# Weight splits spread over the sparse attention, and a rotary half that is exchanged by transfers

## The chip, the cores and the metric

The kernel runs on one core of a Trainium2 chip. A core has TensorE (PE, matrix products into PSUM), VectorE (DVE), ScalarE (ACT), GpSimd (POOL) and SyncE (SP, which here issues DMA transfers). The metric is the device time of one execution in microseconds; "before" stands at a median of 795.12 us over three runs (794.58 to 796.4).

## The reference, cut to what matters

The program is one decoder layer over 1024 tokens of width 1024: a modulated RMS norm, one input projection, two attention groups and an output projection. The second group is a multi-head latent attention with 8 heads; its queries come from a latent of rank 256, and 32 of each head's 96 query dimensions carry a rotary embedding:

```python
def rope(x, pos):
    half = x.shape[-1] // 2
    inv = ROPE_THETA ** (-jnp.arange(half, dtype=jnp.float32) / half)
    ang = pos.astype(jnp.float32)[..., None] * inv
    cos, sin = jnp.cos(ang)[:, :, None, :], jnp.sin(ang)[:, :, None, :]
    x1, x2 = xf[..., :half], xf[..., half:]
    return jnp.concatenate([x1 * cos - x2 * sin, x2 * cos + x1 * sin], axis=-1)

q = (rms_norm(c_q, q_norm_g) @ w_q_up).reshape(B, S, H, 64 + 32)
q_nope = q[..., :64]
q_rot = rope(q[..., 64:], positions)
```

Each output half of the rotary part needs both halves of x: one times the cosine, the other times the sine.

## The kernel before, in words

The kernel keeps float32 accuracy by splitting operands into a high and a low part (hi, and value − hi) and summing three products, hi·hi, hi·lo and lo·hi. A split is an ACT copy to the reduced type followed by a subtraction on DVE or POOL.

It runs in stages: modulation and input projection (to 352 us in the profile), the sparse attention (352 to about 532 us), the latent attention (to about 685 us) and the output projection.

The sparse attention is a loop over 74 pairs of blocks of 128 keys × 512 query columns (four heads). For pair i, `scores` (L994, L995, and L997 for a mask) fills a PSUM slot of tag `s` (three of them), `exps` takes two exponentials of it on ACT (E, float32, L1004; H, float16, L1005), `lows` subtracts them on DVE (L, L1010), and `weigh` multiplies with the values three pairs later (o, L937). A unit (128 tokens, one key group) has three branches, and after each branch `merge` scales the sum (cf, then mixn or tmp on DVE) and POOL adds it (L968). There are two PSUM banks for these sums, so the next branch waits for the merge before it.

Beside the pairs the loop prepares the latent attention with small jobs from three lists:
- `work`, from pair SIDE = 4 on, one each pair: two value/key weight splits (`kv_weights`), a bound on the values (`v_bound`, `v_scale`) and four query weight splits (`q_weights`). Each split job loads its weights into the one buffer of tag `raw`.
- `side`, from pair 36, every second pair: transposes of the latents and of the rotary tables.
- `late`, after pair 44 once `side` is empty: `k_rot`, `q_rot(0, 0)`, `q_rot(0, 1)`, `kq_first` twice, `q_rot_rows`, and the peaks of head 0 (`max_m`, L1256), which need the rotated rows.

`q_weights` stores the rotary columns of the weights twice: in their order, and with the two halves of 16 swapped. `q_rot(grp, hf)` (four heads, 512 tokens) multiplies the latents with both sets, twelve matmuls into the two halves of a PSUM slot (L1225). The first half times the cosine table (L1228), the second times the signed sine table (L1229), their sum on POOL (L1230), and its split into `qrs` (ACT L1231; L1232 on DVE for group 0 and on POOL for group 1) give the rotated rows, four heads × 32 rows × 512 tokens. The two products lie in a tile of the ring of three E tiles in the sparse attention, and in the one tile of tag `kqh` in the latent attention. `q_rot(1, 0)` and `q_rot(1, 1)` are placed at tasks 6 and 7 of the 48 tasks of the latent attention. `kq_first` uses the buffer `raw` and one of tag `rawl`; `kq_up` (L1155, L1156) uses `kqh` and `kql`, which transfers carry on to the heads' tiles.

Only TensorE's order is the order of the code. The instructions of the other engines, and the issues on SP's queue, are ordered by a planner that simulates the program with its own costs; a tile is reused when all that touched it is done. Each engine executes its own list in order, so an instruction that waits holds up those behind it.

Of the kernel before, what the change touches and what calls it, by code (L numbers as in the profile page):

```python
# [22 lines left out]
P = 128  # L23
# [4 lines left out]
H = 8  # L28
# [32 lines left out]
CMP_AT = (1, 12, 20, 28, 30, 44, 52, 60)  # L61
LAG = 3
SIDE = 4
SIDE_LAT = 36
LATE = 44
E_MIX = 8
# [28 lines left out]
def f32(ap):  # L95
    return ap.bitcast(F32)
# [11 lines left out]
def hybrid_block(ctx, tc, x, c, positions, ada_w, ada_b, norm_g, w_in, cmp_pos, cmp_k_w1, cmp_k_w2,  # L108
# [935 lines left out]
    cql = [rpool.tile([P, S], F32R, name=f"cql{k}") for k in range(2)]  # L1044
    wkh, wkl, wvh, wvl = [rpool.tile([P, H, 64], F32R, name=nm) for nm in ("wkh", "wkl", "wvh", "wvl")]
    wnh, wnl = [rpool.tile([P, 2, H, 64], F32R, name=nm) for nm in ("wnh", "wnl")]
    wrh, wrl = [rpool.tile([P, 2, 2, H, 32], F32R, name=nm) for nm in ("wrh", "wrl")]

    def split_w(hi, lo, src):
        nc.scalar.activation(hi, src, AF.Copy)  # L1050
        nc.vector.tensor_tensor(lo, src, f32(hi), op=ALU.subtract)
# [25 lines left out]
    def q_weights(k, i):  # L1077
        hs = slice(4 * i, 4 * i + 4)
        raw = raw_tile(f"wq{k}{i}")[:, :384].rearrange("p (h n) -> p h n", h=4)
        nc.sync.dma_start(raw, w_q_up[0, k * P:(k + 1) * P].rearrange("p (h n) -> p h n", h=H)[:, hs])  # L1080
        split_w(wnh[:, k, hs], wnl[:, k, hs], raw[:, :, :64])
        split_w(wrh[:, k, 0, hs], wrl[:, k, 0, hs], raw[:, :, 64:])
        for j in range(2):
            js = slice(j * 16, (j + 1) * 16)
            split_w(wrh[:, k, 1, hs, js], wrl[:, k, 1, hs, js], raw[:, :, 80 - j * 16:96 - j * 16])

    vb = npool.tile([P, 2], F32, name="vb")

# [127 lines left out]

    def q_rot(grp, hf):
        hs = slice(hf * 512, (hf + 1) * 512)
        pt = slot(f"qr{grp}_{hf}")
        for o in range(2):  # L1220
            n = 0
            for k in range(2):
                wh, wl = [w[:, k, o, grp * 4:grp * 4 + 4].rearrange("p h d -> p (h d)") for w in (wrh, wrl)]
                for a, b in ((wh, cqh[k]), (wh, cql[k]), (wl, cqh[k])):
                    nc.tensor.matmul(pt[:, o * 512:(o + 1) * 512], a, b[:, hs], start=(n == 0), stop=(n == 5))  # L1225
                    n += 1
        t1, t2 = pair_tile(f"qt{grp}{hf}")
        nc.vector.tensor_tensor(t1, pt[:, :512], tab_of[0][:, hs], op=ALU.mult)  # L1228
        nc.vector.tensor_tensor(t2, pt[:, 512:], tab_of[1][:, hs], op=ALU.mult)  # L1229
        nc.gpsimd.tensor_tensor(t1, t1, t2, op=ALU.add)  # L1230
        nc.scalar.activation(qrs[:, 0, hs], t1, AF.Copy)  # L1231
        (nc.gpsimd if grp else nc.vector).tensor_tensor(qrs[:, 1, hs], t1, f32(qrs[:, 0, hs]), op=ALU.subtract)  # L1232

    def v_up(t2):
        pt = slot(f"vu{t2}")
# [131 lines left out]
        nc.gpsimd.affine_select(causal_m[:, 896:], causal_m[:, 896:], pattern=[[-1, P]], compare_op=ALU.is_ge, fill=NEG,  # L1367
                                base=0, channel_multiplier=1)

    def pair_tile(name):  # L1370
        if "l" in mp:
            t = mp["l"].tile([P, 1024], F32, name=name, tag="kqh", bufs=1)
        else:
            t = npool.tile([P, 1024], F32, name=name, tag="E", bufs=EB)
        return t[:, :512], t[:, 512:]

    def junk_tile():
        if "l" in mp:
# [20 lines left out]
    with tc.manual_schedule(engines={mybir.EngineType.PE}):  # L1399
        for i in range(n_pairs + LAG + 2):  # L1400
# [11 lines left out]
            if i < n_pairs:  # L1412
                u = pairs[i][-1][0]
                before = len(todo)
                prep_next(u + 3)
                if u % G == 0 and u // G + 1 < NT and u // G + 1 not in cmr:
                    next_mask(u // G + 1)
                if i in KB_AT:
                    keys_b(kb_late, KB_CUT * P, S, KB_AT.index(i))
                if i >= SIDE and work:  # L1420
                    work.pop(0)()
                elif i >= SIDE_LAT and side:
                    if (i - SIDE_LAT) % 2 == 0:
                        side.pop(0)()
                elif i >= LATE and late and (len(late) > 6 or (i - LATE) % 2):
                    late.pop(0)()
# [164 lines left out]
```

## Time and profile before

| | before |
|---|---|
| median of three runs | 795.12 us |
| the profiled execution | 791.18 us |
| its span, first to last instruction | 789.4 us |
| PE / DVE / ACT / POOL busy | 731.7 / 576.9 / 389.7 / 228.1 us |
| mean granted TensorE clock | 0.976 |
| share of the chain that ended last: PE / DVE / DMA / ACT | 72 / 10 / 7 / 4% |

The profile is of one execution, and its rows add up to that one's own time. Busy time is the time with an instruction under way; matmuls are pipelined, so a row of a matmul is longer than the distance to the next. The chain of waits is followed back from the last instruction to what released each step; a row there is the time for which that instruction held up the end. In the timelines the brackets give the time for which the engine stood idle before the instruction and what ended it. The granted clock is a share of 2.4 GHz. An issue on SP's queue is the time in which SP works on one transfer; the data land later.

### The profile page before, as it was taken

To read this page: it belongs to the slowest core of one execution; us is meant where nothing else is said; L and a number is where in the kernel's file an instruction comes from. 1 tells how busy PE (TensorE), PEld (TensorE's weight loads), DVE (VectorE), ACT (ScalarE), POOL (GpSimd) and SP (SyncE) were. 2 spreads that over 40 slices of the span, in tenths; PEclk is the share of its full clock that TensorE was granted. 3 is DMA by queue.
4 is the path that set the end of the run, shared out by engine and by line. 5 is a ranking of instruction groups with operands and counts; after the bars stand their busy time and mean duration, and the time that the engine had idled before them with its cause. 6 is when DMAs were issued, how large, how long until landed. Compare 5 with 4: busy or idle time off the path is not lost.

```text
span 789.4 us, 17302 instructions
## 1 busy us (share of the span) xinstructions
PE 731.7 (93%) x6464; PEld 647.1 (82%) x6464; DVE 576.9 (73%) x1543; ACT 389.7 (49%) x691; POOL 228.1 (29%) x287
## 2 busy tenths in 40 slices
PE   3899999999999999997899999999698979999996
PEld 3889998998999999995677887777577868888885
DVE  3888835586688788879898989986487888654443
ACT  5545534233223232118899978985355666622112
POOL 3442522155222062404443221120110030054322
PEclk9799999999999999999999999999899999999998
DMA  8953313153431121113321123124315281345431
GB/s 302 300 162 107 94 51 86 61 141 91 137 93 55 31 58 42 35 56 93 80 51 40 33 56 81 36 62 100 77 28 122 58 224 56 145 137 174 152 115 54
DMA packets 62435, 76.48 MB, mean 97 GB/s; under 512 B 6342, under 2 KB 47113, under 8 KB 62351
## 3 DMA queue, kind: packets, MB, share of 16 engines
q1 hardware_dynamic: 57566, 70.91, 31.5%
q10 hardware_dynamic: 4784, 4.47, 1.7%
q8 instruction: 51, 0.84, 0.4%
q14 instruction: 34, 0.27, 0.1%
HBM read 48.33 MB, written 11.53 MB: 76 GB/s over the span
## 4 chain that ended last, share of the span: by engine, by line
PE 72%; DVE 10%; DMA 7%; issue 4%; ACT 4%; POOL 1%; SPq 1%; POOLq 0%; DVEq 0%; ACTq 0%
PE pj L589 23%; PE out L1523 11%; PE o L937 5%; PE pm L841 4%; PE s L994 3%; PE s L995 3%; PE mo L937 2%; PE ms L1297 2%; PE hid L642 2%; DVE L L1010 2%; PE kcT L321 2%; PE ms L1298 2%; PE ms L1299 2%; PE mm L1256 2%; PE qr L1225 1%
## 5 line engine op out<-in xcount | busy, mean ns | idle before, releaser
L589 PE MATMUL pj<-whi,hh 128*128 128x288 f32 (+2 forms) x544 | 161.4, 297 | 0.0
L589 PE MATMUL pj<-wlo,hh 128*128 128x288 f32 (+2 forms) x544 | 158.6, 292 | 0.0
L589 PE MATMUL pj<-whi,hl 128*128 128x288 f32 (+2 forms) x544 | 157.7, 290 | 0.0
L589 PEld LDWEIGHTS pj<-wlo,hh 128*128 128x128 f32 x544 | 102.5, 189 | 1.4
L589 PEld LDWEIGHTS pj<-whi,hh 128*128 128x128 f32 x544 | 102.6, 189 | 0.4
L589 PEld LDWEIGHTS pj<-whi,hl 128*128 128x128 f32 x544 | 102.2, 188 | 0.0
L1010 DVE TENSOR_TENSOR L<-E,H 128x1024 f16<-128x1024 f32 x74 | 92.0, 1243 | 12.8 <-ACT H L1005 10.9
L799 DVE CUSTOM_DVE_ANT_0 junk<-pm,maskw 128x256 bf16<-128x256 f32 (+3 forms) x160 | 77.9, 487 | 16.4 <-PE pm L841 4.4
L1004 ACT ACTIVATE E<-s 128x1024 f32<-128x1024 f32 x74 | 76.4, 1032 | 19.8 <-PE s L995 12.1
L937 PEld LDWEIGHTS <-H 128*128 128x128 f16 x1184 | 57.3, 97 | 30.1 <-issue 17.5
L968 POOL TENSOR_TENSOR mixn<-mixn,tmp 128x256 f32<-128x256 f32 x32 | 44.8, 1401 | 108.7 <-DVE tmp L967 101.8
L1005 ACT ACTIVATE H<-s 128x1024 f16<-128x1024 f32 x74 | 76.2, 1029 | 0.0
L841 PE MATMUL pm<-ka,qall 128*128 128x448 f32 (+5 forms) x208 | 67.2, 323 | 0.2 <-DVE mp L796 0.2
L937 PE MATMUL o<-v,H 128*128 128x65 f16 (+1 forms) x1056 | 60.1, 195 | 4.5 <-DVE mixn L964 4.5
L994 PE MATMUL s<-qa,ka 128*128 128x512 f32 x132 | 57.9, 439 | 3.0 <-ACT H L1005 2.6
L211 POOL TENSOR_TENSOR wlo<-wraw,whi 128x288 fp32r<-128x288 f32 (+2 forms) x64 | 51.4, 828 | 31.6 <-ACT whi L210 27.6
L937 PE MATMUL o<-v,L 128*128 128x65 f16 x528 | 56.8, 193 | 0.0
L937 PEld LDWEIGHTS <-L 128*128 128x128 f16 x592 | 55.7, 100 | 0.0
L1310 ACT ACTIVATE lat<-ms 128x1024 f32<-128x1024 f32 (+2 forms) x40 | 32.7, 817 | 34.2 <-PE ms L1302 16.3
L708 ACT ACTIVATE zt<-pj 128x288 f32<-128x288 f32 (+1 forms) x32 | 12.2, 385 | 74.5 <-PE pj L589 62.4
L1312 DVE TENSOR_TENSOR mL<-lat,mH 128x1024 f16<-128x1024 f32 (+2 forms) x40 | 39.7, 1004 | 5.8 <-ACT mH L1311 5.7
L995 PE MATMUL s<-qall,kb_early 128*128 128x512 f32 x108 | 43.3, 401 | 0.0
(380 smaller groups left out, 1863.5 us busy)
## 6 DMA issues: line engine op xcount, KB each, us to landing
ad<-in_ada_w_dram SPq DMA_DIRECT2D x32, 256.0 KB
wraw<-in_w_in_dram SPq DMA_DIRECT2D x20, 288.0 KB
x<-in_x_dram SPq DMA_DIRECT2D x8, 512.0 KB
gw<-in_ada_w_dram SPq DMA_DIRECT2D x32, 128.0 KB
qa<-qall SPq DMA_DIRECT2D x32, 128.0 KB
wor<-in_w_out_dram SPq DMA_DIRECT2D x16, 256.0 KB
xr<-in_x_dram SPq DMA_DIRECT2D x8, 512.0 KB
out_dram<-y SPq DMA_DIRECT2D x7, 512.0 KB
```

The source lines that it names most:

```text
L211: split.tensor_tensor(wlo[:, :width], raw[:, j, :width], f32(whi[:, :width]), op=ALU.subtract)
L589: nc.tensor.matmul(pt[:, :width], a[k][:, ts], b[:, :width], start=(n == 0), stop=(n == 23))
L799: nc.vector.tensor_tensor_reduce(out=junk[:, :w], in0=scores, in1=mask, scale=1.0, scalar=2.0 * NEG, op0=ALU.add, op1=ALU.max, accum_out=dst)
L841: nc.tensor.matmul(bank[:, :total_w], lhs, keys, start=True, stop=True)
L937: nc.tensor.matmul(po[:, c0:c0 + hi - lo], a[:n, qs], v[:, lo:hi], start=start and j == 0, stop=stop and j == 2, skip_group_check=True)
L968: nc.gpsimd.tensor_tensor(mv, mv, tmp, op=ALU.add)
L994: nc.tensor.matmul(dst, a, staged[u], start=True, stop=False)
L995: nc.tensor.matmul(dst, b, qc[u], start=False, stop=mk is None)
L1004: nc.scalar.activation(Et, pS, AF.Exp, scale=SC_NSA)
L1005: nc.scalar.activation(ph, pS, AF.Exp, scale=SC_NSA)
L1010: nc.vector.tensor_tensor(pl, Et, ph, op=ALU.subtract)
L1523: nc.tensor.matmul(po, a[:, kk], b[hf][k][:, cs.start - hf * 512:cs.stop - hf * 512], start=(n == 0), stop=(n == 23))
```

## The change

Two things are changed. The jobs of the list `work` are issued at every fourth pair (4, 8, ... 32) and no longer at every pair (4 to 11). And `q_rot` computes the rotary part of the queries once, with six matmuls and one set of weights; it multiplies it with the sine table into t2, exchanges neighbouring groups of 16 rows from t2 to t3 with eight transfers on SP's queue, multiplies the same PSUM values with the cosine table (into `qrs`' low half, as a place to keep them) and subtracts t3 on POOL. The sign of the sine table is thereby the other way round, hence the subtraction. In the sparse attention t2 lies in the buffer `raw` and t3 in one of tag `rawl`; in the latent attention both lie in `kqh`. The last subtraction is on DVE for both groups.

```diff
+SIDE_STEP = 4
...
-    wrh, wrl = [rpool.tile([P, 2, 2, H, 32], F32R, name=nm) for nm in ("wrh", "wrl")]
+    wrh, wrl = [rpool.tile([P, 2, H, 32], F32R, name=nm) for nm in ("wrh", "wrl")]
...
-        split_w(wrh[:, k, 0, hs], wrl[:, k, 0, hs], raw[:, :, 64:])
-        for j in range(2):
-            js = slice(j * 16, (j + 1) * 16)
-            split_w(wrh[:, k, 1, hs, js], wrl[:, k, 1, hs, js], raw[:, :, 80 - j * 16:96 - j * 16])
+        split_w(wrh[:, k, hs], wrl[:, k, hs], raw[:, :, 64:])
...
-        pt = slot(f"qr{grp}_{hf}")
-        for o in range(2):
-            n = 0
-            for k in range(2):
-                wh, wl = [w[:, k, o, grp * 4:grp * 4 + 4].rearrange("p h d -> p (h d)") for w in (wrh, wrl)]
-                for a, b in ((wh, cqh[k]), (wh, cql[k]), (wl, cqh[k])):
-                    nc.tensor.matmul(pt[:, o * 512:(o + 1) * 512], a, b[:, hs], start=(n == 0), stop=(n == 5))
-                    n += 1
-        t1, t2 = pair_tile(f"qt{grp}{hf}")
-        nc.vector.tensor_tensor(t1, pt[:, :512], tab_of[0][:, hs], op=ALU.mult)
-        nc.vector.tensor_tensor(t2, pt[:, 512:], tab_of[1][:, hs], op=ALU.mult)
-        nc.gpsimd.tensor_tensor(t1, t1, t2, op=ALU.add)
+        pt = slot(f"qr{grp}_{hf}")[:, :512]
+        n = 0
+        for k in range(2):
+            wh, wl = [w[:, k, grp * 4:grp * 4 + 4].rearrange("p h d -> p (h d)") for w in (wrh, wrl)]
+            for a, b in ((wh, cqh[k]), (wh, cql[k]), (wl, cqh[k])):
+                nc.tensor.matmul(pt, a, b[:, hs], start=(n == 0), stop=(n == 5))
+                n += 1
+        t2, t3 = turn_tiles(f"qt{grp}{hf}")
+        t1 = f32(qrs[:, 1, hs])
+        nc.vector.tensor_tensor(t2, pt, tab_of[1][:, hs], op=ALU.mult)
+        for r in range(0, P, 16):
+            nc.sync.dma_start(t3[r:r + 16], t2[r ^ 16:(r ^ 16) + 16])
+        nc.vector.tensor_tensor(t1, pt, tab_of[0][:, hs], op=ALU.mult)
+        nc.gpsimd.tensor_tensor(t1, t1, t3, op=ALU.subtract)
         nc.scalar.activation(qrs[:, 0, hs], t1, AF.Copy)
-        (nc.gpsimd if grp else nc.vector).tensor_tensor(qrs[:, 1, hs], t1, f32(qrs[:, 0, hs]), op=ALU.subtract)
+        nc.vector.tensor_tensor(qrs[:, 1, hs], t1, f32(qrs[:, 0, hs]), op=ALU.subtract)
...
-    def pair_tile(name):
+    def turn_tiles(name):
         if "l" in mp:
             t = mp["l"].tile([P, 1024], F32, name=name, tag="kqh", bufs=1)
-        else:
-            t = npool.tile([P, 1024], F32, name=name, tag="E", bufs=EB)
-        return t[:, :512], t[:, 512:]
+            return t[:, :512], t[:, 512:]
+        return raw_tile(name), npool.tile([P, 512], F32, name=name + "s", tag="rawl", bufs=1)
...
                 if i >= SIDE and work:
-                    work.pop(0)()
+                    if (i - SIDE) % SIDE_STEP == 0:
+                        work.pop(0)()
```

## Rows read from the trace of the kernel before

**Rows 1.** Stretches: busy us of each engine (instructions), granted clock share, DMA share, GB/s.
```profile
core 0: us, PE busy (x) PEld busy (x) DVE busy (x) ACT busy (x) POOL busy (x), PEclk, DMA share, GB/s
...
399.00:437.00 38.00, 37.99 (x574) 30.15 (x573) 33.80 (x64) 36.64 (x39) 15.10 (x15) 1.00 0.18 46
463.00:480.00 17.00, 16.82 (x147) 13.45 (x144) 13.87 (x18) 10.78 (x13) 4.88 (x4) 1.00 0.13 36
...
560.00:575.00 15.00, 15.00 (x112) 12.76 (x112) 10.88 (x15) 5.28 (x8) 3.43 (x3) 0.89 0.29 69
```

**Rows 2.** Chain of waits, 398 to 456 us: shares of it by line.
```profile
by line: PE o L937 37.0%; PE s L994 25.0%; PE s L995 22.3%; PE s L997 8.1%; PE latT L1095 4.6%; PE tab L1104 1.9%; PE nmT L855 1.3%; issue 0.0%
```

**Rows 3.** ACT in time: start, duration, line, tile; in brackets idle time and releaser.
```profile
362.61 1.08 ACT L1004 ACTIVATE E<-s 128x1024 f32<-128x1024 f32 x1
...
387.65 0.42 ACT L1050 ACTIVATE wnh<-wq 128x256 fp32r<-128x256 f32 x1
...
388.47 1.00 ACT L1004 ACTIVATE E<-s 128x1024 f32<-128x1024 f32 x1
...
390.28 1.02 ACT L1004 ACTIVATE E<-s 128x1024 f32<-128x1024 f32 x1
...
393.23 1.01 ACT L1004 ACTIVATE E<-s 128x1024 f32<-128x1024 f32 x1
...
399.36 1.02 ACT L1004 ACTIVATE E<-s 128x1024 f32<-128x1024 f32 x1 [0.44 <-PE s L995]
...
436.55 1.02 ACT L1004 ACTIVATE E<-s 128x1024 f32<-128x1024 f32 x1
```

**Rows 4.** Chain of waits, 362 to 399 us: start, duration, engine, tile, line.
```profile
378.70 0.88 DVE wnl L1051
379.58 0.47 DVE wrl L1051 x3
...
381.47 0.43 DVE mixn L964
...
389.86 2.53 DMA wq<-in_w_q_up_dram
...
392.75 0.57 ACT wrh L1050 x3
```

**Rows 5.** Chain of waits, whole span: the matmuls of the four rotary calls.
```profile
463.67 2.75 PE qr L1225 x12
468.35 2.83 PE qr L1225 x12
...
563.63 2.83 PE qr L1225 x12
...
569.74 2.87 PE qr L1225 x12
```

**Rows 6.** Instructions on tile qt: count, then shortest, median and longest duration in ns.
```profile
L1230 POOL TENSOR_TENSOR qt<-qt x4: 1279/1284/1287, 467.9 to 574.1; 128x512 f32<-128x512 f32 x4
L1231 ACT ACTIVATE qrs<-qt x4: 634/634/635, 469.5 to 576.4; 128x512 fp32r<-128x512 f32 x4
```

**Rows 7.** Line 1215: issue of one transfer on SP's queue, ns.
```profile
L1215 SPq DMA_DIRECT2D qh<-qrs x6: 553/577/657, 506.1 to 619.1; - x6
```

**Rows 8.** Chain of waits: from the end of an issue to its landing.
```profile
583.52 1.77 DMA qh<-mrow
```

**Rows 9.** SP's queue in time, near the first rotary call.
```profile
464.84 2.91 SPq L859 DMA_DIRECT2D qall<-mr  x4
```

**Rows 10.** TensorE in time: the first peak matmuls.
```profile
486.31 0.71 PE L1256 MATMUL mm<-qall,qall 96*128 96x512 f32 x2
```

**Rows 11.** DVE in time: first product of the second call of group 1.
```profile
572.70 0.69 DVE L1228 TENSOR_TENSOR qt<-qr,lat 128x512 f32<-128x512 f32 x1 [0.41 <-issue]
```

**Rows 12.** Waits, 350 to 690 us: total us, times, longest.
```profile
DVE kql L1156 <- DMA kl<-kql: 12.8, 3, 10.2
...
ACT kqh L1155 <- DMA kh<-kqh: 9.7, 1, 9.7
```

## The prediction

> **What bounds the kernel now.** I read the views from the coarse to the fine: the busy shares of stretches, then the chain of waits of each stretch that the change touches, then single engines in time there. Three stretches matter, and each has another limit. From 362 to 399 us (pairs 4 to 17 of the sparse attention) a pair takes long: E of pair 4 starts at 362.61, of pair 17 at 399.36 and of pair 36 at 436.55 [rows 3], so 13 pairs take 36.75 us, while the next 19 take 37.19 (1.96 each). At the later pace the 13 would take 25.4, so 11.3 us are lost here. The chain there runs largely over DVE and shows where the weight splits sit on it: wnl and wrl for 0.88 + 0.47 us, directly ahead of a merge (mixn at 381.47), and later the load wq, 2.53 us, followed by the ACT copies [rows 4]. From 398 to 456 us the chain is TensorE alone [rows 2], while ACT is nearly full too, 36.64 of 38 us, and DVE is at 33.80 [rows 1]. From 463 to 480 and from 560 to 575 us the rotary calls stand on the chain with their twelve matmuls each, 2.75, 2.83, 2.83 and 2.87 us [rows 5]; TensorE is busy 16.82 of 17 and 15.00 of 15 us there, DVE 13.87 and 10.88 [rows 1].
>
> **The weight splits.** Eight small jobs were issued at pairs 4 to 11; they go to pairs 4, 8, ... 32, so the last is issued ahead of pair 36, where the turns begin: those and the rotary calls keep their pairs. The four query-weight jobs move out of the slow stretch, to pairs 20 to 32. Each loses two small ACT copies and two small DVE subtractions, because the exchanged columns are no longer stored.
> Gain in the slow stretch, by what the chain and ACT show: the merge at 381.47 comes 0.88 + 0.47 = 1.35 us earlier [rows 4]; the ACT copies between 387.65 and 388.47 go, 0.82; and E of pair 14, at 393.23, could follow the two exponentials that begin at 390.28, which like the two from 388.47 take 1.81, so at 392.09, 1.14 earlier [rows 3]. Sum 3.3 us. What is late next is DVE's own series of merges. At least the first term, 1.35, should come; at most the whole pieces of the chain, 1.35 + 2.53 + 0.57 = 4.45 [rows 4]. I take 3.3, since its terms are read where E really starts. The other value-weight jobs stay within the stretch, only later: 0.
> Cost in the middle stretch: of the 0.82 us that a job's four copies take on ACT, two copies remain, with 256 and 128 of 512 columns: 0.41 by their count, 0.62 by columns; I take 0.53. A pair takes 1.96 and two exponentials 1.81, so four pairs leave 0.6 us free: it just fits. DVE has 38 − 33.80 = 4.2 us [rows 1] for four such pairs of subtractions; even at 1.35 each (5.4) little would stick out. The load has four pairs' time and doesn't wait for its buffer. Bounds 0 to 4 × 0.53 = 2.1 if nothing is hidden; I take 0.3. Net of the splits: −3.0.
>
> **The rotary calls.** Each loses six of twelve matmuls, half of its row: (2.75 + 2.83)/2 = 2.79 us in the sparse attention and (2.83 + 2.87)/2 = 2.85 in the latent attention [rows 5]. DVE keeps two products a call, and the two POOL subtractions of group 1 become DVE's. New is the exchange between the products and the addition: eight transfers of 16 rows. The trace has no such transfer; the nearest row, 32 rows of twice the length, occupies SP 0.577 us [rows 7], the lower bound being no issue beyond one, the upper the 0.73 of the issues in [rows 9] (2.91/4). Eight are 4.6 us (0.6 to 5.8), since one queue issues one after the other, and the last lands 1.77 us after its issue [rows 8]. An exchange therefore puts some 6.4 us between product and subtraction.
> Queued behind it: on SP the query loads of later units, on POOL the merge additions, on ACT the split behind which exponentials stand, and on DVE the next call's first product, because both calls now write one buffer (raw, later kqh) instead of a ring of three. Behind that product stand L and the merges, for which TensorE waits.
> *First pair of calls.* The matmuls of the first end by about 465. SP is taken until 464.84 + 2.91 = 467.75 [rows 9], so the issues end at 472.4 and the last lands at 474.1. Then the second product may be written: 474.1 + 0.69, issues to 479.4, landing 481.2, POOL 1.28, ACT 0.63 [rows 6], 483.1; the row transfer 0.58 + 1.77 gives 485.5. The first peak matmul, which needs these rows, runs now at 486.31 [rows 10]. So the longer path is just hidden, with 0.8 us to spare. But the latent key and query splits that follow use the same buffer, free only at 481.2, and hold their PSUM slots meanwhile, so the 2.79 us that TensorE no longer needs become waits for slots. I take 0, between −2.8 and +6.1 (next part).
> *Second pair.* Matmuls from 563.63 to 565.0, product to 565.7, issues to 570.3, landing 572.1, POOL to 573.4. Only then can the next call's first product start, now at 572.70 [rows 11]: 0.7 later instead of earlier. Scores and peaks of the tasks between still come up to 1.4 earlier. I take −0.5, between −2.85 and +5.1.
> The sum: −3.3 + 0.3 + 0 − 0.5 = −3.5. On the profiled execution, 791.18 us (span 789.4 and 1.8 around it), that is 787.7. The median of the timed runs is 795.12, 3.9 above the profiled one; carried over, 791.6.
>
> One page of the Trainium skill, "DMA: Bandwidth & Descriptors" (section "Issuing engines are not separate DMA queues"), says that the sequencer's time to start a DMA is usually small beside the DMA itself. By this trace it is not: 8 × 0.577 against 1.77. By the page an exchange would take little over one landing, and that is the first rival's case.
>
> **The rivals.** *The matmuls pay in full.* If issues are short (the lower bound) an exchange takes 0.6 + 1.77 = 2.4 us, less than one pair and a call, so no slot is held and both halves count: −3.0 − 2.79 − 2.85 = −8.6, 786.5. For it: TensorE is full in both stretches [rows 1]. Against: every SP issue shown is near 0.6 [rows 7].
> *The transfers block an engine (slower).* Only TensorE's order is written by hand; elsewhere a planner orders instructions by its own estimate of when they can run. If it reckons an exchange shorter than it is, the product or split that needs it stands ahead of L or an exponential and blocks them. For it: DVE stood 10.2 and ACT 9.7 us behind transfers out of this very buffer [rows 12]. Against: between SP's issues there is room, and the planner can place these instructions late. Price: 4.6 us a call; in the first pair 9.2 less the 17 − 13.87 = 3.1 us that DVE has free [rows 1], 6.1. Then −3.0 + 6.1 − 0.5 = +2.6, 797.7; with the second pair as well, 9.2 less 15 − 10.88 = 4.1, so 5.1, it is +8.2, 803.3. It turns the sign once the blocking passes some 3.5 us beyond what is free.
> *Nothing to be measured.* The splits come back: only 1.35 is won early and 1.6 of the 2.1 is paid in the middle, the calls come out even: +0.2, 795.3. For it: ACT has 0.6 us free for 0.53. Against: DVE's load in the slow stretch really falls.
>
> **How the numbers follow.** Forecast 0.40, paid in full 0.19, blocked 0.24, nothing 0.17. The likeliest gives 791.6, of itself 789.3 to 793.5. The range reaches to 785.5 (the full payment and 1 us of drift) and to 799.5 (past the first blocked case); outside lie the doubly blocked one and a part of the full payment's spread, under 0.2. About 0.2%, 1.6 us, is what a measurement can tell from no change. Faster by more: 0.58 (forecast without 0.02, paid in full, a little of the last case's spread); within: 0.18; slower: 0.24.
>
> **What would show it.** Right: pair 17 starts its E some 3 us earlier after pair 4, the chain from 398 to 456 us is still TensorE, SP shows eight issues of some 0.58 us a call, each call has six matmuls, and the first peak matmul stands within 1 us of its old distance from the first rotary call. Wrong would be: ACT or DVE rows with idle time ended by the transfers t3; waits of TensorE on the key and query splits longer by more than 3 us; splits of wq on the chain between 400 and 437 us; or issues far shorter than 0.5 us.

## The result and the profile after

The changed kernel takes 804.40 us (median of 16 runs, 796.03 to 808.69) against 796.69 us for the kernel before in the same session; the ratio is 1.0067, 95% interval [1.0043, 1.0091]. It is slower, by some 5.3 us, where 3.5 us less were forecast. The ratios here leave out disturbed runs, the medians hold all. The profiled execution of after took 802.65 us: its span is 800.9 at a mean granted clock of 0.959, where the one of before had 789.4 at 0.976.

I compare stage by stage, by the moments at which ACT begins the exponential E of a pair. The rows are ACT in time in the kernel after (start, duration, line, tile; in brackets the idle time before and what ended it): pairs 4, 17, one weight split, then pairs 36, 47, a key split with the high part H behind it, and pair 54.

```profile
360.21 1.08 ACT L1005 ACTIVATE E<-s 128x1024 f32<-128x1024 f32 x1
...
393.35 1.03 ACT L1005 ACTIVATE E<-s 128x1024 f32<-128x1024 f32 x1 [0.83 <-PE s L996]
...
406.33 0.42 ACT L1051 ACTIVATE wnh<-wq 128x256 fp32r<-128x256 f32 x1 [0.90 <-DMA wq<-in_w_q_up_dram]
...
432.39 1.03 ACT L1005 ACTIVATE E<-s 128x1024 f32<-128x1024 f32 x1
...
458.56 1.02 ACT L1005 ACTIVATE E<-s 128x1024 f32<-128x1024 f32 x1
...
478.17 0.59 ACT L1201 ACTIVATE kqh<-kq 64x512 fp32r<-64x512 f32 x1 [1.58 <-DMA qt01s<-qt]
...
479.71 1.02 ACT L1006 ACTIVATE H<-s 128x1024 f16<-128x1024 f32 x1
...
486.65 1.03 ACT L1005 ACTIVATE E<-s 128x1024 f32<-128x1024 f32 x1 [1.34 <-PE s L998]
```

From pair 4 to 17 it is 33.14 us (36.75 in [rows 3]): 3.61 won. From 17 to 36 it is 39.04 (37.19 in [rows 3]): 1.85 lost, of which 0.90 stands in the row at 406.33, where the split waits for its load. From 47 to 54, the stretch with the first two rotary calls, it is 28.09, where the kernel before takes 26.12: 1.97 lost. Pairs 47 and 54 in ACT's trace of before:

```profile
462.72 1.03 ACT L1004 ACTIVATE E<-s 128x1024 f32<-128x1024 f32 x1
...
488.84 1.03 ACT L1004 ACTIVATE E<-s 128x1024 f32<-128x1024 f32 x1 [1.03 <-PE s L997]
```

SP's queue, the chain of waits and TensorE, all of after, show how; first the queue (start, time, line, tiles, count; the last row spans both calls of the latent attention, with SP's wait between them):

```profile
460.68 2.91 SPq L860 DMA_DIRECT2D qall<-mr  x4
463.69 4.99 SPq L1228 DMA_DIRECT2D qt00s<-qt  x8
...
471.55 5.20 SPq L1228 DMA_DIRECT2D qt01s<-qt  x8
...
565.14 13.97 SPq L1228 DMA_DIRECT2D qt<-qt  x16
```

Then the chain from 462 to 486 us (start, duration, what):

```profile
467.46 0.59 SPq L1228
...
468.09 1.98 DMA qt00s<-qt
...
470.23 1.30 POOL qrs L1230
...
476.16 1.94 DMA qt01s<-qt
...
478.22 1.28 POOL qrs L1230
...
479.52 0.69 DVE kql L1202
...
484.13 1.22 PE mm L1256 x2
```

Where the chain of before was TensorE and its rotary matmuls [rows 5], it is now issue after issue, a landing, POOL, and the same once more: the second call's issues begin only at 471.55, when POOL has read the first call's halves. The second call's product, which writes the buffer that the first exchange reads, stands on DVE behind that exchange's landing (470.07), though its matmuls end by 464.3. Its PSUM slot, one of three, is held until then:

```profile
470.19 0.69 DVE L1226 TENSOR_TENSOR qt<-qr,lat 128x512 f32<-128x512 f32 x1
```

Behind the second exchange stand the key splits: ACT's kqh waits 1.58 us for the landing, and H, which TensorE's next scores need, stands behind kqh on ACT. TensorE in time shows it:

```profile
459.26 0.48 PE L1222 MATMUL qr<-cqh,wrh 128*128 128x512 f32 x1
...
470.67 0.73 PE L1178 MATMUL kq<-cqh,wnh 128*128 128x512 f32 x2 [1.27 <-ACT H L1006]
476.64 0.50 PE L995 MATMUL s<-qa,ka 128*128 128x512 f32 x1 [1.28 <-ACT H L1006]
480.78 0.50 PE L995 MATMUL s<-qa,ka 128*128 128x512 f32 x1 [2.19 <-ACT H L1006]
484.13 1.22 PE L1256 MATMUL mm<-qall,qall 96*128 96x512 f32 x2 [0.16 <-DVE rtab L1202]
```

These are three waits for H, 4.74 us. The middle one is not of the exchange: before has it at the same place, with 1.34 us. The other two make 3.46, more than the 2.79 us of matmuls that the two calls no longer have. TensorE in before, the first rotary matmul and that wait:

```profile
463.43 0.48 PE L1225 MATMUL qr<-cqh,wrh 128*128 128x512 f32 x1
...
482.07 0.50 PE L994 MATMUL s<-qa,ka 128*128 128x512 f32 x1 [1.34 <-ACT H L1005]
```

The first peak matmul of after stands at 484.13, 24.87 us behind the first rotary matmul; before it was 22.88 (from 463.43 to 486.31 in [rows 10]).

In the latent attention the chain of after shows the second pair of calls:

```profile
573.04 0.61 DVE qt L1226
...
578.53 1.94 DMA qt<-qt
...
580.59 2.37 POOL qrs L1230
...
582.98 0.64 ACT qrs L1231
...
583.64 0.69 DVE qrs L1232
584.33 0.07 DVE hl L1270
...
584.55 0.37 PE mn L1272
```

The second call's product starts at 572.96 on DVE, 11.24 us behind the first rotary matmul (561.72). Before it was 9.23 (from 563.47, by its trace, to 572.70 in [rows 11]). Its subtraction at 583.64, which POOL did before, now stands on DVE ahead of hl, for which the peaks' transposition mn waits on TensorE. Two TensorE rows of after name the idle time, and the stretch 565 to 590 us is then set beside the same stretch of before (columns as in [rows 1]):

```profile
574.30 1.32 PE L1256 MATMUL mm<-kh,qh 96*128 96x512 f32 x3 [2.28 <-DVE qrs L1229]
...
584.55 0.37 PE L1272 MATMUL mn<-ident,hl 128*16 128x128 f32 x1 [2.36 <-DVE mcf L1320]
```

After:

```profile
565.00:590.00 25.00, 20.36 (x147) 17.06 (x146) 18.80 (x39) 9.62 (x13) 3.62 (x2) 0.75 0.19 43
```

Before:

```profile
565.00:590.00 25.00, 23.27 (x226) 19.35 (x225) 21.04 (x44) 12.03 (x17) 5.65 (x4) 1.00 0.10 23
```

TensorE is busy for 20.36 us with 147 matmuls, where before it did 226 in 23.27; the granted clock is 0.75, so a good part runs at 1.2 GHz in place of 2.4. The sixth, ninth and twelfth exponential of the latent attention begin on ACT in after at:

```profile
560.61 0.92 ACT L1310 ACTIVATE mixm<-ms 128x896 f32<-128x896 f32 x1 [2.00 <-PE ms L1302]
...
578.22 1.02 ACT L1310 ACTIVATE lat<-ms 128x1024 f32<-128x1024 f32 x1 [1.94 <-PE ms L1299]
...
592.42 0.92 ACT L1310 ACTIVATE lat<-ms 128x896 f32<-128x896 f32 x1 [4.15 <-PE ms L1302]
```

and in before at:

```profile
562.59 0.92 ACT L1310 ACTIVATE mixm<-ms 128x896 f32<-128x896 f32 x1 [2.00 <-PE ms L1302]
...
578.25 1.02 ACT L1310 ACTIVATE lat<-ms 128x1024 f32<-128x1024 f32 x1 [1.23 <-PE ms L1299]
...
587.11 0.92 ACT L1310 ACTIVATE lat<-ms 128x896 f32<-128x896 f32 x1 [2.31 <-DVE peak L1260]
```

From the sixth to the ninth 17.61 us pass (15.66 before), from the ninth to the twelfth 14.20 (8.86). The two profiled spans differ by 11.5 us; 6.19 of these lie behind the twelfth (208.48 us to the end in after, 202.29 in before), where both kernels have the same code, at a granted clock of 0.96 and 0.98.

### The profile page after: what moved, and what is told of

Its sections match the earlier page's. It is cut to its first block, busy times and chain, and to the rows that moved or that the text cites. A ratio compares the mean times of both kernels' runs of the same rounds, so it can differ in the third digit from the quotient of the medians.

```text
span 800.9 us, 17297 instructions
## 1 busy us (share of the span) xinstructions
PE 737.8 (92%) x6440; PEld 653.1 (82%) x6440; DVE 581.1 (73%) x1537; ACT 388.7 (49%) x683; POOL 224.7 (28%) x285
## 4 chain that ended last, share of the span: by engine, by line
PE 72%; DVE 10%; DMA 6%; issue 4%; ACT 4%; SPq 3%; POOL 1%; POOLq 0%; DVEq 0%; ACTq 0%
PE pj L590 24%; PE out L1523 11%; PE o L938 4%; PE pm L842 4%; PE mo L938 3%; PE s L995 3%; PE kcT L322 2%; PE s L996 2%; DVE L L1011 2%; PE mm L1256 2%; PE ms L1297 2%; PE hid L643 2%; PE ms L1298 2%; PE ms L1299 2%; SPq L1228 2%
## 5 line engine op out<-in xcount | busy, mean ns | idle before, releaser
L969 POOL TENSOR_TENSOR mixn<-mixn,tmp 128x256 f32<-128x256 f32 x32 | 42.1, 1316 | 111.5 <-DVE tmp L968 104.9
L1260 DVE CUSTOM_DVE_ANT_0 junkm<-mm,lat 128x1024 bf16<-128x1024 f32 (+7 forms) x48 | 36.2, 753 | 16.5 <-PE mm L1256 16.2
```

Source lines behind the costliest of these rows:

```text
L969: nc.gpsimd.tensor_tensor(mv, mv, tmp, op=ALU.add)
```

## The experiments

All kernels ran against the kernel before on the same chip. The table gives, from each profile, the stages just named (E of pairs 4 to 17, 17 to 36, 47 to 54; latent exponentials 6 to 12), then the mean granted clock of the runs compared, what a kernel takes more or less than before *at like clock*, and the ratio. Like clock comes from a straight line through the 311 runs of the 18 kernels that the comparisons use, with one slope and a level for each kernel: 0.01 of mean clock goes with 5.2 us, 1.7 us scatter about the line, so with 12 runs a level is known to about 1 us, and that of e3, from five runs, to about 1.6. It orders what was seen; it doesn't prove that the clock is the cause. The line pools the runs of before from five chips, whose mean clocks go from 0.964 to 0.969; those beside after's own ratio are not among them. (The expectations of the ninth and later runs quote it from fewer runs.) A dash: no stage is read from that profile.

| kernel | 4-17 | 17-36 | 47-54 | lat. 6-12 | clock | at like clock | ratio [95%] |
|---|---|---|---|---|---|---|---|
| before | 36.75 | 37.19 | 26.12 | 24.52 | 0.966 | 0 | 1 |
| after | 33.14 | 39.04 | 28.09 | 31.81 | 0.960 | +3.2 | 1.0067 [1.0043, 1.0091] |
| e1 splits only | 34.26 | 39.61 | 26.12 | 24.98 | 0.964 | -0.5 | 0.9978 [0.9952, 1.0005] |
| e2 exchange only | 36.09 | 37.51 | 28.52 | 27.66 | 0.963 | +2.9 | 1.0021 [0.9982, 1.0060] |
| e3 no transfers | 33.79 | 38.75 | 23.75 | 23.70 | 0.968 | -5.6 | 0.9883 [0.9834, 0.9932] |
| e4 exchange, latent only | - | - | - | - | 0.966 | -0.7 | 0.9969 [0.9929, 1.0009] |
| e5 exchange, sparse only | 33.42 | 40.20 | 27.89 | 25.76 | 0.965 | +2.3 | 1.0024 [0.9988, 1.0059] |
| e6 two queues | 33.71 | 38.72 | 26.97 | 28.97 | 0.958 | +1.5 | 1.0036 [1.0006, 1.0067] |
| e7 own tile, latent | 33.85 | 38.98 | 29.01 | 26.73 | 0.959 | +2.5 | 1.0056 [1.0019, 1.0093] |
| e8 shuffle | 33.43 | 39.57 | 24.91 | 26.10 | 0.962 | -1.4 | 1.0002 [0.9965, 1.0039] |
| e9 twelve matmuls | 33.45 | 38.80 | 30.12 | 30.24 | 0.961 | +4.7 | 1.0073 [1.0043, 1.0103] |
| e10 shuffle from PSUM | - | - | - | - | 0.965 | -2.7 | 0.9968 [0.9937, 0.9999] |
| e11 loads ahead | 35.35 | 38.04 | 26.12 | 25.72 | 0.970 | +1.8 | 0.9981 [0.9952, 1.0009] |
| e12 unread | 33.13 | 38.94 | 28.40 | 26.16 | 0.962 | -0.7 | 1.0004 [0.9970, 1.0037] |
| e13 own buffers | 34.12 | 39.15 | 27.26 | 26.75 | 0.961 | -0.9 | 1.0047 [1.0012, 1.0083] |
| e14 own buffers, unread | 33.77 | 38.83 | 25.51 | 23.82 | 0.962 | -1.7 | 1.0037 [1.0003, 1.0071] |
| e15 shuffle, loads ahead | 34.04 | 37.80 | 24.84 | 23.62 | 0.964 | -3.7 | 0.9985 [0.9951, 1.0019] |
| e16 issues only | 35.74 | 37.19 | 26.12 | 25.30 | 0.962 | 0.0 | 1.0052 [1.0015, 1.0089] |

**e1, the splits alone.** The kernel before with this:

```diff
+SIDE_STEP = 4
...
-                    work.pop(0)()
+                    if (i - SIDE) % SIDE_STEP == 0:
+                        work.pop(0)()
```

> The kernel before with the work list at every fourth pair, the rotary calls as before. Waiting theory (the exchanges of group 1 cost the time): faster than before by about 1.8 us, the gain that the changed kernel shows at pair 36 of the sparse attention against its first pair, or a little less, since the swapped copies are still split in the middle stretch; ratio 0.997 to 0.999. Splits theory (spreading the splits costs the time): slower, ratio 1.003 or more.

What four pairs win (2.49) the middle gives back (2.42), with all four copies kept. The ratio, 0.9978, is in the range of the waiting theory: the splits are not what makes the change slower.

**e2, the exchange alone.** The kernel after with `SIDE_STEP = 1`.

> The changed kernel with the work list at every pair again. Waiting theory: slower than before, by the loss of the changed kernel and about the 1.8 us that the spread of the splits gave, less about 1 us for the copies no longer made: ratio 1.006 to 1.010. Splits theory: equal to before or faster, ratio 0.996 to 1.001.

The stretch from 47 to 54 is that of after (28.52), the latent one, 27.66, lies between before and after. The ratio, 1.0021, is below what was expected and its interval holds no change too: inconclusive by time, though at like clock it is 2.9 us over before.

**e3, no transfers.** The second table's product is subtracted unexchanged, so the rotary part is left out of what is computed:

```diff
-        for r in range(0, P, 16):
-            nc.sync.dma_start(t3[r:r + 16], t2[r ^ 16:(r ^ 16) + 16])
...
-        nc.gpsimd.tensor_tensor(t1, t1, t3, op=ALU.subtract)
+        nc.gpsimd.tensor_tensor(t1, t1, t2, op=ALU.subtract)
```

> The changed kernel without the eight transfers of each call: t2 itself is subtracted, so the rotated rows are not the right ones and the exchange is left out. Waiting theory: the loss goes, and the halved matmuls pay at least in part, 2 to 8 us faster than before: ratio 0.990 to 0.998. Theory that fewer matmuls let TensorE's clock fall: the clock in the latent attention stays as low as in the changed kernel (0.72 to 0.76 between 560 and 600 us), ratio 1.003 or more.

This is the decisive run: 1.2% under before, even below the waiting theory's range, and 1.8% under after. Pairs 47 and 54 in its trace:

```profile
460.12 1.02 ACT L1005 ACTIVATE E<-s 128x1024 f32<-128x1024 f32 x1
...
483.87 1.02 ACT L1005 ACTIVATE E<-s 128x1024 f32<-128x1024 f32 x1 [1.16 <-PE s L998]
```

23.75 us: the six matmuls a call pay 2.37 us there, near the 2.79 counted for them, and the exchange takes 28.09 - 23.75 = 4.34 away (4.14 to 5.26 by the profiles of e2, e5 and e7, whose calls there are those of after). The other theory wanted a granted clock of 0.72 to 0.76 between 560 and 600 us; with six matmuls a call and no transfers it is 1.00 (0.74 in after, 0.96 in before).

**e4 and e5, the exchange in one pair of calls.** The other pair keeps the code of before, with its exchanged weight columns:

```diff
+        if grp not in EXCH:
+            return q_rot_two(grp, hf)
```

> The changed kernel with the exchange in group 1 alone (latent attention); group 0 (sparse attention) with twelve matmuls and both sets of weights as before. Waiting theory: as slow as the changed kernel or 1 to 2 us better, ratio 1.004 to 1.008, with the low clock between 560 and 600 us. If the exchange in the sparse attention were the cause: equal to before or faster, 0.996 to 1.001.

> The exchange in the calls of the sparse attention only; the two calls in the latent attention keep twelve matmuls, two products and POOL as before (the splits of their weights keep the exchanged columns). Theory 1 (the waiting behind the exchanges of the sparse attention is the larger part of the loss, 4.4 us in the stretch from pair 47 to pair 54, and the kernel with the exchange in the latent attention alone came out at 0.997): ratio to the kernel before 1.003 to 1.008, pair 47 to 54 about 28 us, the latent attention's ninth E again 49 us after the last sparse one. Rival (the latent attention is where it is lost, for 2.1 us there and the low clock behind it): ratio 0.995 to 1.000. If neither half alone is slower than before, the loss needs both: ratio also under 1.001, with the stretch from 47 to 54 at 28 us all the same.

e4 missed: with the exchange in the latent attention alone the time is that of the splits alone (-0.7 and -0.5 at like clock). e5 confirms the place: 27.89 us from 47 to 54, and 2.8 us more than e1 at like clock, though its ratio is below the 1.003 of theory 1. But neither is clearly slower than before, and their mean clocks are near that of before; only both together are slower, with a lower clock.

**e6, two queues.** `(nc.scalar if r % 32 else nc.sync).dma_start(...)` in place of `nc.sync.dma_start(...)`.

> Of the eight transfers of each exchange every second one is issued by ACT's queue in place of SP's. Theory 1 (the serial issue on one queue, 8 x 0.59 us, is the larger part of the 6.7 us between product and subtraction): the issues take 2.4 us in place of 4.7, the path 4.3, the stretch from pair 47 to 54 falls from 28.1 to about 25 us, ratio 0.998 to 1.002. Rival (ACT is nearly full there, so four issues of some 0.6 us in each call cost ACT the 2.4 us that SP saves, and an issue that waits for the product blocks the exponentials behind it): ratio 1.005 to 1.012 and ACT's idle time behind the issues grows.

SP's issues took 2.52 us for four in the first call, but only about 1.1 us of the stretch come back; the time lies between both expectations, above that of before.

**e7, own tile in the latent attention.** The second call takes the tag kql, the first keeps kqh.

> The second rotary call of the latent attention writes its products into another buffer than the first (that of the low key and query parts), so that its product need not wait until the first call's subtraction is done. Theory 1 (the two calls in series, on one buffer, make the 2.1 us by which the ninth latent E is late, and the low clock behind it): second call's product about 4 us earlier, SP's issues then directly behind those of the first, ninth E at 49.5 to 50 us, ratio 1.001 to 1.004. Rival (SP's queue keeps the order anyway and the later splits wait for the other buffer in the same way): ninth E at 51, ratio 1.005 to 1.009.

Rows of the sixth and ninth latent exponential:

```profile
570.15 0.92 ACT L1310 ACTIVATE mixm<-ms 128x896 f32<-128x896 f32 x1 [2.01 <-PE ms L1302]
...
583.74 1.02 ACT L1310 ACTIVATE lat<-ms 128x1024 f32<-128x1024 f32 x1 [1.24 <-PE ms L1299]
```

13.59 us in place of 17.61: the shared buffer is what delays the ninth, as theory 1 said. The time hardly moved all the same (1.0056, in the rival's range); from the ninth to the twelfth 13.14 us pass, at a granted clock of 0.79 in that trace from 584 to 600 us.

**e8 and e10, a shuffle in place of the transfers.** The first permutes the product, the second the matmuls' result, and POOL then multiplies:

```diff
-        for r in range(0, P, 16):
-            nc.sync.dma_start(t3[r:r + 16], t2[r ^ 16:(r ^ 16) + 16])
+        nc.vector.stream_shuffle(t3, t2, [r ^ 16 for r in range(32)])
...
+        nc.vector.stream_shuffle(t3, pt, [r ^ 16 for r in range(32)])
+        nc.gpsimd.tensor_tensor(t2, t3, tab_of[1][:, hs], op=ALU.mult)
+        nc.gpsimd.tensor_tensor(t1, t1, t2, op=ALU.add)
```

> The halves are exchanged by one VectorE shuffle a call (each block of 32 partitions permuted) in place of the eight transfers; all else as in the changed kernel. Theory 1 (the loss is the 6.7 us path of issues and landing, nothing in the six matmuls): by the products' 0.69 us a shuffle costs about 0.7 us of DVE, four of them 2.8 at most on the path, so ratio 0.988 to 0.994, near the kernel without an exchange (0.988), pair 47 to 54 at 24 to 25 us, and TensorE's clock without the drop after 560 us. Rival 1 (fewer matmuls and the splits' new places lose the time, the transfers only show it): ratio above 1.000. Rival 2 (the shuffle is much slower than a product, 2 us or more): DVE the bound there, ratio 0.996 to 1.002.

> The exchange by one VectorE shuffle that reads the matmuls' result itself; POOL then multiplies by the second table and adds, two instructions of 1.28 us, so DVE has two instructions a call ahead of POOL as before the change, and not three. Theory 1 (the 0.73 us of DVE a call, four calls, are most of what parts the kernel with shuffles, 1.8 us under the kernel before at like clock, from the one without an exchange, 6.1 under it): 3 to 5 us under the kernel before at like clock, ratio 0.992 to 0.998. Rival (POOL's path, longer by 1.28 us, keeps the rows of the peaks late): 0 to 2 us under it, ratio 0.998 to 1.002.

The shuffle in e8's trace (VectorE in time):

```profile
467.32 0.73 DVE L1227 STREAM_SHUFFLE qt00s<-qt 128x512 f32<-128x512 f32 x1
```

0.73 us for what took some 7 by transfers; the stretch is 24.91 us. At like clock e8 lies 4.6 us under after, but its ratio, 1.0002, is above the 0.994 that theory 1 allowed and in the range of both rivals; the stretch is as theory 1 had it, and the shuffle isn't slow, as rival 2 wanted. e10 comes to 0.9968, as theory 1 had it, and to 2.7 us under before at like clock, a little less than the 3 to 5 expected; it is the only kernel that still does the exchange and whose interval lies below 1.

**e9, twelve matmuls.** Each of the six once more into the unused half of the slot.

> The changed kernel with the six matmuls of each rotary call done twice, the second time into the unused half of the same PSUM slot, whose result nobody reads: TensorE's work of before, the exchange of after. Over all runs so far the time follows the mean granted clock by 5.7 us for 0.01; at like clock the changed kernel is 2.5 us longer than before, and 3.2 us more come from its clock, 0.959 against 0.964. Theory 1 (the clock falls because the exchange makes TensorE wait, whatever its work): clock 0.957 to 0.960 again, and the time at like clock 2 to 8 us above the changed kernel's, ratio 1.008 to 1.016. Rival (the clock falls because TensorE has fewer matmuls): clock back at 0.963 to 0.966, ratio 1.003 to 1.008.

Inconclusive: the ratio, 1.0073, lies in the rival's range, the clock, 0.961, between the two, and at like clock the kernel is 1.5 us over after where theory 1 asked for 2 to 8. What TensorE's lighter work does to its clock isn't settled by it.

**e11, loads ahead.** e1 with each load two pairs ahead of its split and the query loads in two buffers:

```diff
+    work = [lambda f=f, i=i: f(i) for i in range(2) for f in (kv_load, kv_weights)] + [v_bound, lambda: None, v_scale]
+    work += [lambda f=f, k=k, i=i: f(k, i) for k in range(2) for i in range(2) for f in (q_load, q_weights)]
```

> Only the spreading of the splits, as in the kernel with the splits alone (pairs 4 to 32, all copies kept), but each weight load is issued two pairs ahead of its splits, the query loads alternately into two buffers. Theory 1 (the 1.9 to 2.4 us that the splits cost between pairs 17 and 36 are ACT and DVE waiting for a load issued at the same moment, 0.90 us at one of them): the 19 pairs from 17 to 36 take 37.5 to 38.2 us in place of 39.6, ratio 0.994 to 0.998. Rival (it is the work of the copies on a nearly full ACT): they take 39 us or more, ratio 0.997 to 1.000.

38.04 us from 17 to 36 in place of 39.61, as theory 1 said: by this stretch 1.57 of the 2.42 that the splits cost there are waiting for the load. In time it brought nothing: from 4 to 17 it takes 1.09 more than e1, the ratio, 0.9981, is the same and lies in the rival's range, and at like clock it is 2.3 us over e1, for which no run shows a reason.

**e12 to e14, who holds whom.** e12 issues all transfers, but POOL subtracts t2 and not t3, so the exchange is left out of what is computed, as in e3. e13 reads them, from buffers that no other call shares; e14 does both, with e12's subtraction and these buffers:

```diff
-            t = mp["l"].tile([P, 1024], F32, name=name, tag="kqh", bufs=1)
-            return t[:, :512], t[:, 512:]
-        return raw_tile(name), npool.tile([P, 512], F32, name=name + "s", tag="rawl", bufs=1)
+            t = mp["l"].tile([P, 1024], F32, name=name, tag=("kqh", "kql")[int(name[-1])], bufs=1)
+        else:
+            t = npool.tile([P, 1024], F32, name=name, tag="E", bufs=EB)
+        return t[:, :512], t[:, 512:]
```

> All 32 transfers are issued as in the changed kernel, but POOL subtracts the product itself and not the exchanged one, so that nothing of the row path waits for a landing; only the buffers are still held by the transfers. Theory 1 (the path through the exchange, product to issue to landing to POOL, is what is paid): the stretch from pair 47 to 54 falls from 28.1 to 24 to 25.5 us, ratio 0.990 to 0.997. Rival (SP's 0.59 us an issue delays what is queued behind them, the rows of the masks and of the queries, or the held buffer blocks the second call and the key splits): the stretch stays at 27 us or more, ratio above 1.000.

> The products of every rotary call get a buffer that no other call shares: in the sparse attention one of the ring of the exponentials, as before the change, in the latent attention kqh for the first and kql for the second call. Transfers and their order stay. Theory 1 (the held buffer is what is paid in the sparse attention): the stretch from pair 47 to 54 falls from 28.1 us to 25 to 26.5, the ninth latent E stands at 47 to 48, ratio 0.996 to 1.002. Rival (SP's issues delay what is queued behind them): the stretch stays at 27.5 to 29 us, ratio 1.003 to 1.008. Second rival (a buffer of the ring that is held for some 7 us is missing to the exponentials): 29 us or more, ratio above 1.006.

> The same buffers, and POOL subtracts the product itself in place of the exchanged one, so that the transfers are issued and land without a reader. What is left of the exchange is SP's 32 issues of 0.59 us. Theory 1 (the buffer): 24 to 25.5 us from pair 47 to 54, like the kernel without transfers (23.7), ratio 0.989 to 0.995. Rival (SP): 27 us or more there, ratio above 0.999. If e13 stays at 28 and this one falls to 25, it is the path through the landing after all.

Pairs 47 and 54 in e14's trace, then its queue, and its first peak matmul on TensorE:

```profile
461.66 1.02 ACT L1005 ACTIVATE E<-s 128x1024 f32<-128x1024 f32 x1
...
487.17 1.02 ACT L1005 ACTIVATE E<-s 128x1024 f32<-128x1024 f32 x1 [1.78 <-PE s L998]
```

```profile
466.79 10.98 SPq L1228 DMA_DIRECT2D qt<-qt  x16
477.87 0.54 SPq L1204 DMA_DIRECT2D kq_dram<-kqh  x1
...
482.66 0.59 SPq L1213 DMA_DIRECT2D qall<-qrs  x1
```

```profile
485.11 0.70 PE L1256 MATMUL mm<-qall,qall 96*128 96x512 f32 x2 [2.02 <-DMA qall<-qrs]
```

Without a reader the stretch is 28.40 us, with own buffers 27.26, with both 25.51. The four kernels that have the calls of after there lie from 27.9 to 29.0, so neither alone does much and both together do: the wait for the landing and the wait for the shared buffer cover each other, and whoever takes away one finds the other. What the buffer holds is seen on DVE: the second call's product starts 8.37 us behind the first call's in after and in e12, but 3.38 and 3.65 behind it in e13 and e14. The first of after's three waits for H, 1.27 us, is still there in e12 and gone in e13 and e14. In the latent attention each alone does more (26.16 and 26.75, against 31.81 in after and 27.66 in e2), and both together come to 23.82, with 23.70 without transfers. The 1.8 us by which e14's stretch stays above e3's go with SP: sixteen issues in a row keep it for 10.98 us, the rows of the queries, qall, are issued only at 482.66, and the first peak matmul waits 2.02 us for their landing (2.57 in e13), where in e3 it waits for nothing. The ratios agree with the rivals all the same: 1.0004 for e12, 1.0047 and 1.0037 for e13 and e14, with clocks of 0.961 and 0.962.

**e15, shuffle and loads ahead**, the edits of e10 and e11 together.

> The shuffle that reads the matmuls' result, joined with the weight loads issued two pairs ahead of their splits. If the two gains add: 0.3% of the one (0.9968) and the 1.6 us by which the loads ahead shorten the pairs from 17 to 36 against the splits alone, so ratio 0.993 to 0.997, faster than both kernels. Rival (the splits with half of their copies have no stall left that a load ahead could take away): 0.996 to 0.999.

The last three stages are the shortest or near it, and at like clock it is 3.7 us under before; the ratio, 0.9985, is not told apart from 1 and lies in the rival's range, so that the two gains add is not shown. Against the kernel after it is faster by more than both intervals.

**e16, the issues alone.** The kernel before with eight transfers a call added, from latent values to a spare buffer:

```diff
+        t3 = spare_tile(f"qx{grp}{hf}")
+        for r in range(0, P, 16):
+            nc.sync.dma_start(t3[r:r + 16], f32(cqh[0])[r ^ 16:(r ^ 16) + 16, hs])
```

> The kernel before, with eight transfers of the same size added at the place of each rotary call on SP's queue, from latent values that are long there into a spare buffer that nobody reads; splits, matmuls, products and the row path as before. Theory 1 (SP's issues alone, 4.7 us a call, delay the rows queued behind them): the stretch from pair 47 to 54 grows from 26.1 to 27 to 28 us, 1 to 3 us over the kernel before at like clock; if they also are what lowers the clock, the mean over the runs falls to 0.958 to 0.962, together ratio 1.003 to 1.008. Rival (issues only cost where something waits for them): 25.8 to 26.4 us, clock 0.963 to 0.966, ratio 0.998 to 1.001.

In the sparse attention SP issued the first calls' transfers between other work from 441 us on, the last at 464.70, and the stretch is unchanged at 26.12 us: the rival. Since these transfers need no product, they never stood ahead of the rows, as those of after and e14 do; what issues cost at that place is shown by e14 and not here. At like clock nothing clear is lost either (0.0, and 1.0 against the runs of before on its own chip), yet the ratio is 1.0052, with the clock at 0.962 and that chip's before at 0.968: the other half of theory 1. An issue that nobody waits for costs no path here, but the time was lost all the same.

## Why the prediction was wrong, point by point

- **Early splits, -3.3:** right; 3.61 us were won between pairs 4 and 17.
- **Middle, +0.3:** mis-sized; it is 1.85 (its upper end was 2.1). A load of wq stands on the chain of after at 403.77, for 2.54 us, the sign of being wrong that the prediction named. What failed is "The load has four pairs' time and doesn't wait for its buffer": a job issues its load and its split at the same moment, so the split stands on ACT in front of the exponentials until the load lands. Of the two ends, the one in which nothing is hidden was nearly right.
- **First pair of calls, 0:** this is the step that failed in the main. The exchange's size was right: 4.99 us of issues for the 4.6, 1.98 of landing for the 1.77, and from the moment at which SP is free 6.5 us to the landing (463.59 to 470.07) for the 6.35 reckoned (467.75 to 474.1). Only the second call's issues were reckoned too early, by the 0.67 us from the end of its product to POOL's end on the first exchange (470.88 to 471.55). "So the longer path is just hidden" was not: the first peak matmul stands 1.99 us further behind the first rotary matmul, and the stretch is 1.97 us longer. The prediction followed the row path alone and named the splits that wait for the same buffer, but priced them at no more than the matmuls saved. In the runs the exchange cost 4.34 against a saving of 2.37. So the rival in which the transfers block an engine had the mechanism of this stretch: ACT's kqh stood 1.58 us for a landing with H behind it. Its 6.1 for the pair was too much, its sign was right.
- **Second pair, -0.5:** wrong in the profile; 1.95 us are lost to the ninth exponential. The second product came 2.0 us later, not 0.7; one of these comes from the first call's matmuls, which ran 2.48 us for six, partly at 1.2 GHz (the granted clock is 0.60 from 560 to 565 us), where 1.4 was reckoned. That the two calls share a buffer was seen (kqh is shared before the change, too; new is that transfers hold it); that TensorE would wait 2.28 us for the slot and 2.36 behind DVE's subtraction was not. In the timed runs, though, this exchange alone cost nothing (e4), so they don't refute the -0.5.
- **The clock** has no term in the sum. By the line through the runs the kernel after is 3.2 us longer at like clock, and its clock, 0.960 against 0.966, goes with 3.5 more (together more than the 5.3 of the ratio, whose runs of before the line doesn't hold). The four stage terms give -3.61 + 1.85 + 1.97 + 1.95 = +2.2, near the first part; so the sum lost its sign on its own terms. What the profile loses beyond them, 5.34 us from the ninth to the twelfth latent exponential (with the wait of 2.36 among them) and 6.19 behind it, comes at a lower clock.
- **What stays open:** what lowers the clock. Every kernel that has transfers in both pairs of calls lies between 0.958 and 0.963, with waits (after, e6) or nearly without (e14, e16); those with one pair at 0.965 and 0.966; e3 and e11 at 0.968 and 0.970. But of those without transfers e8 lies at 0.962, e1, e15 and e10 at 0.964 and 0.965. Fewer matmuls, waits and transfers each fit some of this; no run settles the mean. In one stretch the profiles say more, one of each kernel: from 575 to 590 us the granted clock is 1.00 in before, e3, e14 and e16, but 0.61 in after and 0.77 in e9. Neither the matmuls (six a call in e3, e14 and after, twelve in the others) nor the transfers (none in before and e3) sort these; TensorE's waits between 570 and 590 us do: 2.28 and 2.36 us in after, 1.62 and 1.25 in e9, none over 1.05 in the four. Yet e14 and e16 have a mean of 0.962.

On the page of the Trainium skill "DMA: Bandwidth & Descriptors" (section "Issuing engines are not separate DMA queues") the sequencer's share of a DMA is usually small: for these transfers the trace still disagrees, with 0.59 us an issue and 4.99 for eight in series beside a landing of 1.98. The same sentence says that several issuing engines save that share alone; e6 agrees, with 2.52 us for SP's four issues in place of 4.99 for eight.

## What to carry to other kernels

Before you replace matmuls by transfers, count the issues of their queue one after the other, add the landing, and then follow the buffer that the transfer reads or writes: whoever writes it next pays the same path, and an engine in whose order that instruction stands pays for everything behind it. A wait that is taken away and brings nothing may have a second one beside it, so try both at once (e12 to e14) before calling it innocent. And look for the same movement on an engine: one VectorE shuffle did in 0.73 us what eight transfers did in 7.

## What the runs showed of the hardware

- An issue on SP's queue took 0.59 us for a transfer of 32 KB between partitions (after), the last one landing 1.94 to 1.98 us after its issue; sixteen in a row took 10.98 us (e14).
- A shuffle of 128 x 512 f32 within blocks of 32 partitions took 0.73 us on VectorE (e8), against 0.68 for a product of that size.
- The mean granted clock differs from run to run of one kernel (0.953 to 0.973 in after), and time goes with it by 5.2 us for 0.01, over 311 runs. A part of this lies outside of what was edited: the first E begins at 352.4 us in the profile of after and at 360.4 in that of e11, behind the same code, and from the twelfth latent exponential to the end, the same code again, it is 201.2 us in e12 and 209.1 in e14. Two profiles of one execution each are therefore best compared by stage, not by their spans.
- In the latent attention of after TensorE's score matmuls began 0.23 us apart at 570 us and 0.43 apart at 575 to 577, at the lower level (granted clock 0.50), behind an idle time of 2.28; the granted clock of 575 to 600 us is 0.67.
